# A transformer block on one core whose instruction order is chosen by another scheduler model

## The chip, the core and the metric

The kernel runs on one core of a Trainium2 chip. The metric is the device time of one execution in microseconds (us), from runs of the kernel alone. The engines of the core are TensorE (PE, matrix products; PEld is its weight load), VectorE (DVE), ScalarE (ACT), GpSimd (POOL) and SyncE (SP), which here issues nearly all DMA transfers. Each engine takes its instructions in the order of its own queue; an instruction that needs the result of another engine or of a transfer waits at the head of its queue.

## The reference

One layer of a hybrid encoder block, in float32, for one sequence of 2048 tokens with 1024 features:

```
xn = RMSNorm(h)
[mLSTM cols | MLA cols] = xn @ W_in
y_A = bidirectional chunkwise mLSTM   (4 heads x 128, chunks of 128)
y_B = multi-head latent attention     (4 heads, v dim 128)
h  += concat(y_A, y_B) @ W_out
h  += GatedMLP_with_centred_dwconv(RMSNorm(h))      (hidden size 2816)
h  += sigmoid(RMSNorm(h) @ W_g) * RMSNorm(p @ W_p)
out = RMSNorm(h)
```

The attention is a full softmax over 2048 keys for each of 4 heads and 16 tiles of 128 queries. The mLSTM runs over 16 chunks in both directions.

## The kernel before

Matrix products are done in several parts: a float32 operand is split into a rounded high part (a cast on ScalarE, L121) and the rest (a subtraction on VectorE, L124), and each product is a sum of products of such parts. So ScalarE and VectorE have two operations for each operand tile that PE uses.

The stages in the order of the program, with their place in the profiled execution:

- the input projection, 0 to 187 us (L134, L283); pairs of the convolution for the mLSTM's queries and keys, 187 to 425 (L544); the attention's queries, 425 to 480 (L860 on), whose order on PE is written by hand;
- the attention, 480 to 1180. For each head and tile of queries: four banks of scores on PE (L1162, tiles `bk`), their maxima on VectorE (L1195, `mx`), the negated maximum of the four (L1206, `nm`), the exponential of each bank on ScalarE with its row sums (L1212, `pe`, which frees the bank), transposes on PE (L1262, `tb`), the split of the transposed tile (L121 and L124, `pt`), and the product with the values (L1247, `ppv`). A bank is reused for the scores of a later tile once the exponential has read it. Between these steps the mLSTM's work is woven in by a generator: masks and states (L1017 to L1033, L1105 to L1154; `kk`, `cf`, `mk`, `mb`, `hy`, `qi`, `den`), and, at the end, the preparation of the output projection: its weights' splits (`op` from `opr`) and its first operands (`fw`, `fwd` from `yr`);
- the stream, 1180 to 2839: 84 pairs of 84 matmuls (L1740, results `fx`, `fy`, `fz`), 8 pairs for the output projection, 44 for the up projection, 24 for the down projection, 8 for the last gate. The last pair's order on PE, VectorE and ScalarE is written by hand (L1963).

The output of the attention is divided by the row sums only in `Out.scale` (L2007 to L2009): the reciprocals of the row sums (L1218, L1219, `gt`) are turned by PE (L1309, `tb`), copied by ScalarE (L1311, `ri`), stored (L1312, `ri_d`), loaded again for 128 partitions (L148, `rb`), and multiplied on VectorE onto the loaded attention output (L2003 loads `yr`, L2009 multiplies). L1695, L1696, L1713 and L1714 then form sums and differences of the `yr` tiles of a pair.

What sets the order: the code gives the instructions in program order, and a scheduler in the build re-orders them region by region before they are put into the engines' queues. It goes by its own model of how long an instruction takes. Left as written are the regions in `manual_schedule` (PE in the queries, L839; ScalarE in the last tile of the attention, L1340; PE, VectorE and ScalarE in the last pair of the stream, L1963) and single instructions pinned by `keep_in_program_order`. PE's instructions in the attention are tied together one by one:

```
def chained(self, ins):
    if self.link:
        self.tc.add_manual_dep(ins.ins, self.link.ins.name, mybir.DependencyInfo(
            mybir.DependencyClass.NoSync, mybir.DependencyReason.DATA), reason="chained")
    self.link = ins
```

so the scheduler may put other PE work (mLSTM, the stream's first products) between them, but not exchange them. The program order of an attention tile is a word list, "s" for a bank of scores, "X" for the negated maximum, "e" and "E" for an exponential, "t" for transposes and a split, "V" for the product with the values, and a dot for one step of the side work:

```
order = "s0 E1 . s1 E2 . . t0 t1 . . s2 . E3 . s3 . . X e0 t2 t3 . . V . .".split()
```

## Time and profile before

| | us |
|---|---|
| three runs, median (lowest to highest) | 2839.11 (2837.26 to 2842.2) |
| the profiled execution | 2840.89 |
| its span, first to last instruction | 2838.7 |
| PE busy, of the span | 2805.3 |
| VectorE busy | 2123.5 |
| ScalarE busy | 1574.3 |

The span is what the trace shows of the profiled execution; 2.2 us of that execution's time lie around it. The granted clock of PE was 0.998 of full speed on average. In the rows of a timeline the first number is the start in us from the beginning of the span, the second the duration; a bracket names the idle time ahead of the instruction and what ended it. In the table by windows, each engine's busy time is followed by its number of instructions, then come the granted clock of PE, the busy share of the DMA engines and GB/s.

### The profile page before, as it was taken

Reading aid. Unit: us, or ns where it says so; the run is one execution under the profiler, and the core shown is the slowest. Engines: PE = TensorE matmul, PEld = TensorE weight load, DVE = VectorE, ACT = ScalarE, POOL = GpSimd, SP = SyncE. Lnnn points to the kernel's source line nnn. Section 1 sums busy time; section 2 is a strip of 40 time slices with the busy share of each in tenths; the row PEclk is TensorE's granted clock in tenths of the full one; section 3 lists DMA queues with packets and bytes.
Section 4 is the critical chain, followed back from the end, with each engine's and each line's share of the span. In section 5 each row is a group of like instructions: output and inputs, shape, how many; then the busy total and the mean of one; then the engine's idle time right before and its main releaser. Section 6 shows DMA issues by size and latency. Waiting matters only on the chain.

```text
span 2838.7 us, 39453 instructions
## 1 busy us (share of the span) xinstructions
PE 2805.3 (99%) x13756; PEld 2349.9 (83%) x13756; DVE 2123.5 (75%) x3597; ACT 1574.3 (55%) x3068; POOL 209.3 (7%) x331
## 2 busy tenths in 40 slices
PE   9999999999999999999999999999999999999998
PEld 7888887888888888788888888888888788888787
DVE  4867866778777777877778778777778766676777
ACT  6346775566565556655655556655556332254665
POOL 2100000000000000044100000000000000011012
PEclk9999999999999999999999999999999999999999
DMA  8974756554433334588645445567776757575864
GB/s 299 289 236 120 216 183 216 190 175 140 136 129 106 99 99 128 160 255 288 224 154 195 163 163 187 184 208 237 227 239 215 223 195 234 170 267 200 294 199 163
DMA packets 444207, 553.73 MB, mean 195 GB/s; under 512 B 34500, under 2 KB 294632, under 8 KB 444008
## 3 DMA queue, kind: packets, MB, share of 16 engines
q1 hardware_dynamic: 444008, 551.21, 60.1%
q8 instruction: 108, 1.77, 0.3%
q14 instruction: 91, 0.75, 0.1%
HBM read 358.50 MB, written 192.61 MB: 194 GB/s over the span
## 4 chain that ended last, share of the span: by engine, by line
PE 90%; DVE 4%; DMA 3%; ACT 1%; issue 1%; SPq 0%; POOL 0%; POOLq 0%; ACTq 0%; DVEq 0%
PE fy L1740 22%; PE fz L1740 14%; PE fx L1740 14%; PE bk L1162 9%; PE bk L134 6%; PE ppv L1247 6%; PE tb L1262 4%; PE fy L544 3%; PE fx L544 2%; PE fz L544 2%; PE fs L134 1%; PE mb L1124 1%; PE mb L1029 1%; PE mb L1125 1%; DVE op L124 1%
## 5 line engine op out<-in xcount | busy, mean ns | idle before, releaser
L1740 PE MATMUL fz<-op,fw 128*128 128x512 f32 x1968 | 478.9, 392 | 2.0 <-DVE ug L1725 2.0
L1740 PE MATMUL fy<-op,fw 128*128 128x512 f32 x1968 | 475.3, 390 | 1.7 <-DVE xt L1725 1.4
L1740 PE MATMUL fx<-op,fw 128*128 128x512 f32 x1968 | 476.2, 390 | 0.0
L1740 PEld LDWEIGHTS fz<-op,fw 128*128 128x128 f32 x1968 | 368.6, 188 | 79.5 <-DVE ug L1725 2.4
L1740 PEld LDWEIGHTS fy<-op,fw 128*128 128x128 f32 x1968 | 368.6, 188 | 79.0 <-DVE xt L1725 1.8
L1740 PEld LDWEIGHTS fx<-op,fw 128*128 128x128 f32 x1968 | 368.2, 188 | 76.2
L1162 PE MATMUL bk<-kv,q_t 128*128 128x512 f32 x1280 | 334.8, 402 | 2.6 <-DVE q_t L1179 1.4
L1162 PEld LDWEIGHTS bk<-kv,q_t 128*128 128x128 f32 x1280 | 228.5, 188 | 45.5 <-ACT pe L1212 2.2
L121 ACT CAST pt<-tb 128x512 fp32r<-128x512 f32 x256 | 139.8, 588 | 183.5 <-PE tb L1262 183.2
L1740 PE MATMUL fy<-op,fwd 128*128 128x512 f32 (+1 forms) x984 | 237.9, 390 | 2.6 <-DVE fh L1725 1.5
L1195 DVE TENSOR_REDUCE mx<-bk 128x1 f32<-128x512 f32 x256 | 174.9, 686 | 58.2 <-PE bk L1162 55.3
L1740 PEld LDWEIGHTS fy<-op,fwd 128*128 128x128 f32 x984 | 182.6, 188 | 41.4 <-DVE fh L1725 1.9
L1247 PE MATMUL ppv<-pt,kv 128*128 128x512 f32 (+1 forms) x1024 | 198.7, 343 | 1.0 <-DVE pt L124 1.0
L1212 ACT ACTIVATE pe<-bk,nm 128x512 f32<-128x512 f32 x256 | 174.3, 697 | 34.5 <-DVE nm L1206 34.3
L124 DVE TENSOR_TENSOR pt<-tb,pt 128x512 fp32r<-128x512 f32 x256 | 167.8, 684 | 32.5 <-ACT pt L121 31.0
L124 DVE TENSOR_TENSOR fw<-fwr,fw 128x1024 fp32r<-128x1024 f32 x124 | 151.0, 1221 | 35.2 <-ACT fw L121 35.1
L1247 PEld LDWEIGHTS ppv<-pt,kv 128*128 128x128 f32 x1024 | 156.0, 188 | 20.3 <-DVE pt L124 1.2
L121 ACT CAST op<-opr 128x512 fp32r<-128x512 f32 x201 | 117.1, 619 | 75.2 <-PE fy L1740 12.7
L121 ACT CAST fw<-fwr 128x1024 fp32r<-128x1024 f32 x124 | 129.8, 1051 | 37.9 <-DVE fwr L1714 20.6
L124 DVE TENSOR_TENSOR op<-opr,op 128x512 fp32r<-128x512 f32 x201 | 131.5, 693 | 23.4 <-ACT op L121 23.3
L1262 PE MATMUL tb<-ident,pe 128*128 128x128 f32 x1024 | 135.5, 273 | 0.1
L121 ACT CAST fw<-hraw 128x1024 fp32r<-128x1024 f32 (+1 forms) x72 | 70.2, 980 | 114.8 <-PE fx L1740 58.9
(399 smaller groups left out, 4444.1 us busy)
## 6 DMA issues: line engine op xcount, KB each, us to landing
fwr<-in_w_up SPq DMA_DIRECT2D x66, 512.0 KB, 4.8
fh<-h_d SPq DMA_DIRECT2D x48, 512.0 KB, 4.2
h_d<-fh SPq DMA_DIRECT2D x48, 512.0 KB, 4.4
s_d<-fwr SPq DMA_DIRECT2D x44, 512.0 KB, 3.2
fws<-s_d SPq DMA_DIRECT2D x44, 512.0 KB, 3.5
rw<-row_d SPq DMA_DIRECT2D x32, 512.0 KB, 4.9
tw_d<-tsum SPq DMA_DIRECT2D x60, 256.0 KB, 5.1
opr<-tw_d SPq DMA_DIRECT2D x60, 256.0 KB, 4.6
```

Of the source, the lines that this page charges most:

```text
L121: nc.scalar.copy(hi, src)
L124: (sub or nc.vector).tensor_tensor(lo, src, _f(hi), op=ALU.subtract)
L134: mm = lambda *a, **k: self.nc.tensor.matmul(*a, **k, skip_group_check=more)
L544: nc.tensor.matmul(out, a[:, k * P:(k + 1) * P], parts[lo], start=first, stop=lo == 1 and k == 3, skip_group_check=more)
L1029: mm(ps[:, i, 0:129], kw[:, h, :], v1[:, h, :], start=True, stop=True)
L1124: mm(ps[:, i, 0:129], mk2[:, r, h, :], v1[:, h, :], start=True, stop=False)
L1162: mm = lambda *a, **k: self.chained(nc.tensor.matmul(*a, **k))
L1195: nc.vector.tensor_reduce(s.mx[:, kb:kb + 1], ps, axis=AX.X, op=ALU.max)
L1212: nc.scalar.activation(s.pe[:, kb % 2], s.banks[kb], AF.Exp, bias=s.nm, accum_out=s.rs[:, kb:kb + 1])
L1247: mm = lambda *a, **k: self.chained(nc.tensor.matmul(*a, **k))
L1262: self.chained(nc.tensor.transpose(t[:, j, :], s.p[kb][:, j * P:(j + 1) * P], self.ident))
L1740: nc.tensor.matmul(out, a[:, k * P:(k + 1) * P], parts[lo][:, cols], start=first, stop=lo == 1 and k == last, skip_group_check=more)
```

## The change

The tile framework's context is opened with another argument. It makes the scheduler go by the build's timeline simulation, another model of the machine, where it chooses which instruction comes next.

```diff
-    with _tile.TileContext(nc) as tc:
+    with _tile.TileContext(nc, schedule_with_timeline_sim=True) as tc:
         body(tc, d)
```

The instructions are the same, apart from one load of a table of ScalarE's functions that falls away (15 rather than 16). Regions ordered by hand keep their order. Everywhere else each engine's queue, SyncE's with the transfers included, is put in a new order, and with it the banks and buffers that rotate. Three places follow.

ScalarE near the end of the attention (`pe_11565` is the exponential of the first two banks of a tile, `ri_11606` the copy of the row sums' reciprocals, `mk_11664` masks of the mLSTM). Before:

```order
L1105 ACTIVATE mk_11664<-mk_11664,cols_2247 128x128 x4
L1145 ACTIVATE hy_11359,dsq_11553<-hy_11359 128x128 x4
L1105 ACTIVATE mk_11664<-mk_11664,cols_2247 128x128 x2
L121 CAST pt_11512<-tb_11513 128x4x128
L121 CAST pt_11520<-tb_11521 128x4x128
L1105 ACTIVATE mk_11664<-mk_11664,cols_2247 128x128 x2
L121 CAST op_12132<-opr_12009 128x512
L121 CAST pt_11567<-tb_11568 128x4x128
L121 CAST pt_11575<-tb_11576 128x4x128
L1212 ACTIVATE pe_11565,rs_11564<-bk_11495,nm_11562 128x512
```

Now:

```order
L121 CAST pt_11575<-tb_11576 128x4x128
L121 CAST q_t_11609<-q_t_11609 128x256
L1145 ACTIVATE hy_11359,dsq_11553<-hy_11359 128x128 x2
L1279 COPY ya_11601<-ppv_11473 128x256
L1311 COPY ri_11606<-tb_11604 32x128
L1105 ACTIVATE mk_11664<-mk_11664,cols_2247 128x128 x8
L121 CAST op_12132<-opr_12009 128x512
L1145 ACTIVATE hy_11359,dsq_11553<-hy_11359 128x128 x2
L1212 ACTIVATE pe_11565,rs_11564<-bk_11495,nm_11562 128x512
L1212 ACTIVATE pe_11565,rs_11564<-bk_11503,nm_11562 128x512
```

The mLSTM's masks and the copy of `ri` now stand ahead of the exponentials; before, the exponentials came directly behind the splits and the copy of `ri` behind them.

VectorE at the same place, from the split of `op_12132` on (`yr_11998` is the first attention output that is scaled, `rb_11994` its row sums' reciprocals; `mx_11611` the maxima of the next tile). Before, L2009 on `yr_11998` stood eight operations behind `nm_11704`, the negated maximum of that tile:

```order
L124 TENSOR_TENSOR op_12132<-opr_12009,op_12132 128x512
L1219 RECIPROCAL gt_82<-gt_82 128x1
L1148 TENSOR_TENSOR hy_11359<-hy_11359,rsr_11560 128x512
L124 TENSOR_TENSOR q_t_11609<-q_t_11609 128x256
L1195 TENSOR_REDUCE mx_11611<-bk_11612 128x1
L1284 TENSOR_TENSOR ya_11601<-ya_11601,ppv_11473 128x256
L1195 TENSOR_REDUCE mx_11611<-bk_11623 128x1
```

Now:

```order
L124 TENSOR_TENSOR op_12132<-opr_12009,op_12132 128x512
L2009 TENSOR_TENSOR yr_11998<-yr_11998,rb_11994 128x512
L1033 SCALAR_TENSOR_TENSOR cf_11490<-cf_11123,cols_2247,mb_11540 128x129 x2
L1148 TENSOR_TENSOR hy_11359<-hy_11359,rsr_11560 128x512
L1195 TENSOR_REDUCE mx_11611<-bk_11612 128x1
L1284 TENSOR_TENSOR ya_11601<-ya_11601,ppv_11473 128x256
L124 TENSOR_TENSOR op_12043<-opr_12001,op_12043 128x512
L1195 TENSOR_REDUCE mx_11611<-bk_11623 128x1
```

L2009 has moved ahead of all four maxima of the tile. Some 60 rows further on, `nm_11945` (the negated maximum of a later tile) likewise has operations of the output projection ahead of it that stood behind it: `fw1_12161`, `fwd_12195`, L1695, L1696 and L1713 on the `yr` tiles, `fw1_12248`, `op_12132`, `op_12171` and `pt_11848`.

VectorE at the end of the attention (`pt_12301` is the last split that the attention's last product needs, `yr_12594` an attention output of a later pair). Before:

```order
L124 TENSOR_TENSOR pt_12293<-tb_12361,pt_12293 128x4x128
L124 TENSOR_TENSOR op_12368<-opr_12219,op_12368 128x512
L2009 TENSOR_TENSOR yr_12508<-yr_12508,rb_12510 128x512
L124 TENSOR_TENSOR pt_12301<-tb_12379,pt_12301 128x4x128
L1218 TENSOR_REDUCE gt_82<-rs_12290 128x1
```

Now:

```order
L2009 TENSOR_TENSOR yr_12508<-yr_12508,rb_12510 128x512
L124 TENSOR_TENSOR pt_12293<-tb_12361,pt_12293 128x4x128
L124 TENSOR_TENSOR op_12368<-opr_12219,op_12368 128x512
L124 TENSOR_TENSOR fwd_12561<-yr_12508,fwd_12561 128x512
L2009 TENSOR_TENSOR yr_12594<-yr_12594,rb_12596 128x512
L1695 TENSOR_TENSOR yr_12508<-yr_12508 128x512
L124 TENSOR_TENSOR pt_12301<-tb_12379,pt_12301 128x4x128
```

L2009 on `yr_12594`, which before stood 37 rows further on, is now ahead of `pt_12301`. On SyncE the load of its `rb_12596` and that of `rb_12724` have moved ahead of the operand loads `opr_12415` and `opr_12419`.

## The prediction

> **What bounds the kernel now.** The page comes first: the span, the busy shares of the engines, and the chain that ended last.

> ```profile
> span 2838.7 us, 39453 instructions
> ...
> PE 2805.3 (99%) x13756; PEld 2349.9 (83%) x13756; DVE 2123.5 (75%) x3597; ACT 1574.3 (55%) x3068; POOL 209.3 (7%) x331
> ...
> PE 90%; DVE 4%; DMA 3%; ACT 1%; issue 1%; SPq 0%; POOL 0%; POOLq 0%; ACTq 0%; DVEq 0%
> ```

> TensorE (PE) is busy 99% of the span, and 90% of the chain is its own work. No matmul is added or removed, so the time can only change through PE's idle time (and its clock). VectorE (DVE) at 75% is next. Then the table by stage, PE's busy time first in each row, and the sum.

> ```profile
> 1100.00:1110.00 10.00, 10.00 (x62) 8.80 (x61) 7.75 (x21) 8.32 (x29) 1.20 (x2) 1.00 0.40 122
> 1110.00:1120.00 10.00, 10.00 (x66) 8.87 (x65) 8.66 (x18) 6.14 (x16) 0.00 (x0) 1.00 0.64 224
> 1140.00:1150.00 10.00, 10.00 (x57) 8.29 (x56) 9.68 (x19) 6.16 (x15) 0.00 (x0) 1.00 0.53 158
> ```
> ```profile
> 1400.00:2200.00 800.00, 799.82 (x3529) 662.14 (x3528) 618.14 (x751) 445.57 (x633) 0.00 (x0) 1.00 0.60 196
> 2800.00:2838.70 38.70, 29.45 (x142) 24.68 (x140) 28.43 (x44) 17.81 (x39) 7.86 (x17) 0.92 0.43 144
> sum 2838.70, PE 2805.32 PEld 2349.92 DVE 2123.46 ACT 1574.26 POOL 209.25; mean PE 187.02 PEld 156.66 DVE 141.56 ACT 104.95 POOL 13.95
> ```

> PE is idle 2838.70 - 2805.32 = 33.4 us in all, 38.70 - 29.45 = 9.25 of them in the last stretch, which is ordered by hand. So an order can win at most about 24 us. It can lose far more: at the end of attention PE has no idle time only because VectorE, busy 7.75 to 9.68 of each 10 us, hands over in time. Last, the view of PE's waits, the total per line and the longest one:

> ```profile
> PE mb L1029 <- DVE kk L1022: 2.5, 1, 2.5
> PE fz L1740 <- DVE ug L1725: 2.0, 1, 2.0
> PE fy L1740 <- DVE xt L1725: 1.9, 2, 1.4
> PE mb L1153 <- DVE hy L1148: 1.8, 4, 0.9
> PE fy L1740 <- DVE fh L1725: 1.5, 1, 1.5
> ```

> No single wait is large; the kernel loses little anywhere.

> **The change part by part.** The instructions stay (one table load of ScalarE fewer); only their places in the queues move. I went along the queues and compared how much work now stands ahead of each hand-over to PE. In the steady part of the stream (1400 to 2200) products and conversions move together, and I cost them at nothing: VectorE idles 800 - 618 = 182 us there, and that cover would have to vanish first. In most of the attention VectorE's work between two hand-overs shifts by several us, but earlier banks cover it; nothing again. Two places are left where the new order looks worse, and two where it looks better.

> *Term A, 1108 to 1130.* The rows of ScalarE, PE, VectorE and SyncE there:

> ```profile
> 1101.30 1.28 ACT L1105 ACTIVATE mk<-mk,cols 128x128 f32<-128x128 f32 x4
> ...
> 1109.04 0.70 ACT L1212 ACTIVATE pe<-bk,nm 128x512 f32<-128x512 f32 x1
> ...
> 1111.96 0.25 ACT L1311 COPY ri<-tb 32x128 f32<-32x128 f32 x1
> ```
> ```profile
> 1111.09 0.27 PE L1309 MATMUL tb<-ident,gt 128*32 128x128 f32 x1
> 1111.12 2.56 PE L1162 MATMUL bk<-kv,q_t 128*128 128x512 f32 x10
> ...
> 1122.58 2.47 PE L1162 MATMUL bk<-kv,q_t 128*128 128x512 f32 x10
> ```
> ```profile
> 1119.47 0.15 DVE L1206 TENSOR_REDUCE nm<-mx 128x1 f32<-128x4 f32 x1
> ...
> 1121.66 0.68 DVE L2009 TENSOR_TENSOR yr<-yr,rb 128x512 f32<-128x512 f32 x1
> ```
> ```profile
> 1112.23 0.34 SPq L1312 DMA_DIRECT2D ri_d<-ri  x1
> ...
> 1114.83 0.38 SPq L148 DMA_DIRECT2D rb<-ri_d  x1
> ```
> ```profile
> DMA to landing us min/median/max: 3.3/4.7/6.2
> ```

> First ScalarE. Before, the exponential (1109.04) ran as soon as its maximum was there; now the copy of `ri` (needs PE's L1309), eight L1105 (2 x 1.28 = 2.6 us), one split and two square sums (about 1 us) stand ahead of it. With L1309 ending at 1111.4 and four matmuls of L1125/L1124 moved ahead of it (0.9), the copy ends at about 1112.5, the exponential starts at about 1116. PE's scores at 1111.12 need the bank that it frees, so PE stands for about 3 us. Then VectorE. Its L2009 on `yr_11998`, at 1121.66 before, is now ahead of four maxima and of `nm` (1119.47). It waits for two loads of `rb`, which follow the store of `ri` at 1112.23. In the old order the first was issued at 1114.83; in the new one no store stands between, so about 1114.2, and with the median landing of 4.7 it arrives at 1118.9. VectorE stands from about 1112 to then, with some 8.7 us of work (nine operations of 0.68, two of 1.29 or less) left before `nm`: 1128 rather than 1119.5. PE's scores at 1122.58 wait for the exponential behind it, now at about 1128.5 to 1129: 6 us late, the 3 us above within them. **A = +6**; bounds 0 (the stall is only a shift of idle time) and +9 (all of `nm`'s delay).

> [...]

> *Term B, 1131 to 1160.*

> ```profile
> 1143.19 0.15 DVE L1206 TENSOR_REDUCE nm<-mx 128x1 f32<-128x4 f32 x1
> ...
> 1144.58 1.21 DVE L124 TENSOR_TENSOR fw<-yr,fw 128x1024 fp32r<-128x1024 f32 x1
> ```
> ```profile
> 1143.43 0.69 ACT L1212 ACTIVATE pe<-bk,nm 128x512 f32<-128x512 f32 x1 [0.48 <-DVE nm L1206]
> ```
> ```profile
> 1144.26 2.58 PE L1162 MATMUL bk<-kv,q_t 128*128 128x512 f32 x10
> ```

> `nm` at 1143.19 feeds the exponential at 1143.43, whose end (1144.12) frees the bank for PE's scores at 1144.26: a slack of 0.14 us. Nine operations of the out projection's preparation, behind this `nm` before, stand ahead of it now: seven of about 0.68 and two of 1.21, 7.2 us by their rows, while one of 0.68 goes behind it. Since neighbouring rows overlap a little I take 5.5 of the 6.5, less about half a us that earlier hand-overs give. **B = +5**; bounds 0 (VectorE makes up for it in PE's new idle time from A) and +8.

> *Term C, 1175 to 1210, attention's last product and the first out-projection pairs.*

> ```profile
> 1177.81 0.69 DVE L2009 TENSOR_TENSOR yr<-yr,rb 128x512 f32<-128x512 f32 x1
> 1178.42 0.68 DVE L124 TENSOR_TENSOR pt<-tb,pt 128x512 fp32r<-128x512 f32 x1
> ...
> 1204.83 0.69 DVE L2009 TENSOR_TENSOR yr<-yr,rb 128x512 f32<-128x512 f32 x1
> ```
> ```profile
> 1179.20 1.63 PE L1247 MATMUL ppv<-pt,kv 128*128 128x512 f32 x8
> ```

> The L2009 of `yr_12594`, at 1204.83 before, now stands ahead of the split `pt` at 1178.42. Its load waits for the L2009 that ends at 1178.5, and needs 4.7 (up to 6.2): the split moves to 1183.8 at least, and PE's product at 1179.20 with it, +5. About 12 matmuls pulled ahead on PE cover 2.9. On SyncE a second `rb` load that waits for this L2009 stands ahead of the operand loads of the next pairs; they come some 3 us later. **C = +4**; bounds 0 (more matmuls pulled ahead) and +10 (no cover, operands late as well).

> *Term D, better places.* The wait of 2.0 on `ug` goes: the product that it needs is 11 us earlier. It costs more than itself:

> ```profile
> 2205.00:2210.00 5.00, 3.86 (x18) 2.85 (x16) 5.00 (x8) 2.49 (x5) 0.00 (x0) 1.00 0.83 256
> 2210.00:2215.00 5.00, 4.17 (x11) 3.30 (x12) 3.71 (x6) 3.14 (x5) 0.00 (x0) 0.66 0.82 268
> ```
> ```profile
> 2204.62 2.88 PE L1740 MATMUL fx<-op,fw 128*128 128x512 f32 x12
> ...
> 2210.84 4.60 PE L1740 MATMUL fz<-op,fw 128*128 128x512 f32 x12 [1.98 <-DVE ug L1725]
> ```

> After that wait the granted clock was 0.66, and twelve matmuls took 4.60 instead of 2.88: 1.7 more. So 3.7 are to be had, and 1.5 from the wait on `fh` (2660 to 2668). Against that stand about 2 us at 495 to 510, where the mLSTM chain of products and copies is now packed closer on PE than its copies allow. **D = -3**; bounds -8 (half of the other waits go as well) and +2.

> *Term E, the clock.* The same rows give the price of a stall's aftermath, 1.7 us. Other waits as long (2.5 on `kk`) left the clock alone, so of the three or four stalls of A to C I count one and a half: **E = +2.5**; bounds 0 and +7.

> [...]

> Sum against the profiled execution (2840.89, span 2838.7): 2840.9 + 6 + 5 + 4 - 3 + 2.5 = 2855.4. It was 1.8 above the median of the three runs, 2839.11, so I predict **2854**.

> **The rivals.**
> - *No change.* VectorE idles a quarter of the span, and what is pulled ahead is done and need not be done later; A to C shrink to the loss of one bank, 1 to 2 each, and D pays for them: 2840.9 + 4 - 3 - 1.8 = 2840. For it: most of the attention shows that slack. Against: the slack of 0.14 at 1144. That the change did nothing is excluded: the listings of VectorE's queue, some 3,100 rows each, differ in 4,793 lines.
> - *Faster.* The mechanism is at PE's own waits, not at VectorE: the new order spaces producer and consumer wider. It decides if half of the 24 us of idle time that isn't hand-ordered is closed, while the `rb` loads land before VectorE gets to L2009, that is if some 7 us of its other work runs in front of it by then. A and B are then under 1: 2839.1 - 12 + 3 = 2830. Against: in the new queue that work stands behind L2009, not ahead.
> - *Far slower.* The head-of-line waits seen in A recur all over the attention: 64 softmax steps (256 maxima in fours), and if one in four loses 1.4 us, as the longest wait on `xt` does, 22 more: 2876. For it: the conversions of the queries now stand closer behind their loads. Against: those have several us of slack in the middle of the attention.

> **How the numbers follow.** Forecast 0.52, with its own range 2844 to 2866; no change 0.18; faster 0.13; far slower 0.17. The range leaves out the lower half of the faster case and the upper part of the far slower one, about 2 in 10: 2833 to 2880. A measurement of this kernel tells about 0.2% (5.7 us) from no change; the forecast's case gives a little to "same": faster 0.13, same 0.19, slower 0.68.

> **What would show it.** Right: PE idle in the windows 1110 to 1130 and 1140 to 1165 rises from nothing to some 5 us each, with L2009 shown as waiting for a DMA of `rb` and PE's L1162 for the exponential of L1212; 1170 to 1210 loses 4 more than before; the wait on `ug` is gone; 1400 to 2200 stays full. Wrong: those windows stay full (A and B are hidden), or idle time turns up in windows of the attention from 500 to 1080 that I cost at nothing, or VectorE waits in the stream.

## The result and the profile after

| | before | after |
|---|---|---|
| median (lowest to highest), us | 2839.99 (2837.26 to 2842.2) | 3006.72 (3002.34 to 3010.41) |
| ratio to before, 95% interval | | 1.0593 [1.058, 1.0605] |
| span of the profiled execution | 2838.7 | 3008.5 |
| PE busy / idle in the span | 2805.3 / 33.4 | 2864.6 / 143.9 |

The change makes the kernel 167 us slower, far outside the range that was given (2833 to 2880). The page of the kernel after: span, busy shares, and the chain by engine.

```profile
span 3008.5 us, 39537 instructions
...
PE 2864.6 (95%) x13756; PEld 2388.5 (79%) x13756; DVE 2122.4 (71%) x3597; ACT 1572.8 (52%) x3067; POOL 218.2 (7%) x331
...
PE 74%; DMA 9%; DVE 7%; ACT 3%; issue 2%; SPq 0%; POOL 0%; ACTq 0%; POOLq 0%; DVEq 0%
```

VectorE and ScalarE do the same work in the same time as before; PE has 110.5 us more of idle time, and the same 13756 matmuls are busy for 59.3 us more. Together that is the 169.8 us between the spans. Next the table by windows, of the kernel after: each engine's busy time, then (behind POOL's) PE's granted clock.

```profile
600.00:800.00 200.00, 165.42 (x934) 140.52 (x933) 122.43 (x290) 87.21 (x243) 9.41 (x14) 0.88 0.38 119
800.00:1000.00 200.00, 180.57 (x1043) 155.42 (x1042) 132.95 (x317) 101.75 (x295) 14.97 (x21) 0.93 0.33 103
1000.00:1180.00 180.00, 155.72 (x873) 133.93 (x873) 112.83 (x276) 87.92 (x257) 14.11 (x20) 0.91 0.29 90
...
1600.00:1800.00 200.00, 200.00 (x884) 165.62 (x883) 155.31 (x196) 105.41 (x148) 0.00 (x0) 1.00 0.51 172
```

and the first of these windows before:

```profile
600.00:800.00 200.00, 199.73 (x1250) 175.98 (x1249) 158.32 (x386) 120.47 (x348) 15.89 (x24) 1.00 0.42 135
```

From 600 to 800, where PE was full, it now does 934 instead of 1250 matmuls, and up to 1180 its granted clock is 0.88 to 0.93. The stream (1600 to 1800) is as full as before. So the loss is in the middle of the attention, the place that the prediction had costed at nothing; idle time there is the sign that it had named for being wrong. The view of PE's waits names it:

```profile
PE mb L1029 <- DVE hy L1136: 34.2, 15, 3.3
PE mb L1029 <- DVE cf L1033: 10.5, 15, 0.7
PE ppv L1247 <- DVE ya L1284: 9.3, 3, 5.4
PE mb L1029 <- DVE kk L1022: 8.2, 5, 2.6
...
PE mb L1029 <- DVE cb L1033: 7.1, 6, 4.0
```

Fifteen waits on `hy` and fifteen on `cf`: one of each in every chunk of the mLSTM's forward loop that updates a state. One such place on PE after (start, duration; in brackets the idle time before and what ended it):

```profile
883.31 0.39 PE L1125 MATMUL mb<-cb,qi 128*128 128x129 f32 x2
883.45 1.30 PE L1247 MATMUL ppv<-pt,kv 128*128 128x512 f32 x6
887.83 1.20 PE L1029 MATMUL mb<-v,kk 128*128 128x129 f32 x4 [3.08 <-DVE hy L1136]
889.73 1.23 PE L1029 MATMUL mb<-v,kk 128*128 128x129 f32 x4 [0.70 <-DVE cf L1033]
890.61 3.93 PE L1162 MATMUL bk<-kv,q_t 128*128 128x512 f32 x10
```

and the state products of a chunk before:

```profile
638.95 0.61 PE L1029 MATMUL mb<-v,kk 128*128 128x129 f32 x4
639.32 1.40 PE L1162 MATMUL bk<-kv,q_t 128*128 128x512 f32 x5
640.56 0.49 PE L1262 MATMUL tb<-ident,pe 128*128 128x128 f32 x3
640.88 0.61 PE L1029 MATMUL mb<-v,kk 128*128 128x129 f32 x4
```

L1029 doesn't use `hy` or `cf`; neither is an operand of it. But every product of the mLSTM (L1017, L1029, L1110, L1124, L1125, L1153) writes a tile `mb` from a pool of PSUM with a single buffer, `("ml", 1)` in `run`. So the next product waits until the last one's result has been read out of that bank, here by VectorE: in L1136 for `hy`, in L1033 for `cf`. At the place above the read by L1136 ends at 887.69 and L1029 starts at 887.83; that by L1033 ends at 889.68, and the second pair starts at 889.73. Before, five matmuls of the attention or more stood between the two pairs of L1029 of a state, and the bank was read while they ran (by L1033 from 640.09 to 640.69, between the pairs at 638.95 and 640.88). After, the two pairs are next to each other on PE. The listings of PE's order, counted over the forward and the backward loop (matmuls of other kinds between the two pairs of L1029 of one state):

```
            states   fewest between   none between   median
before        30           5                0            9
after         30           0               20            0
```

This table is about the wait on `cf`. The larger one, on `hy`, is of the first pair, which follows the last L1125 on the bank. In the traces 18 other matmuls or more stand between these two before (23 in the median), and after it depends on the chunk: in ten of the 15 chunks there are 0 to 6, and the wait is 2.6 to 3.3 us; in the other five there are 15 to 25, and it is 0.4 to 0.8.

What a stall costs behind itself is to be seen in the rows too: ten matmuls of L1162 take 3.93 us at 890.61, where the granted clock is 0.50 up to 893.59, and 2.49 to 2.56 at 903.86 to 918.05, where it is 1.00. The backward loop is hit in another way. After, its last chunks were left over, and stand in a row with no work of the attention between them:

```profile
620.46 0.66 PE L1017 MATMUL mb<-ident,kTb 128*128 128x128 f32 x4 [0.70 <-DVE cb L1033]
622.52 0.71 PE L1029 MATMUL mb<-v,kk 128*128 128x129 f32 x4 [1.40 <-DVE kk L1022]
623.93 1.23 PE L1029 MATMUL mb<-v,kk 128*128 128x129 f32 x4 [0.70 <-DVE cb L1033]
625.86 1.12 PE L1017 MATMUL mb<-ident,kTb 128*128 128x128 f32 x4 [0.70 <-DVE cb L1033]
```

Where the time went in the span: the starts of PE's matmuls of L134, L544, L1162, L1247 and L1740, the k-th of them in the trace after less the k-th before. The differences of that delay, from stretch to stretch (times are those of before; the delay jumps at some of the boundaries, so a row is good to some 1.5 us):

```
 before, us      delay added, us    what runs there
   0 -  480          +6.9           input projection, pairs, queries
 480 -  606         -12.8           backward loop (part of it deferred)
 606 -  666         +47.8           its rest, in a row on PE
 666 - 1043         +74.3           forward loop
1043 - 1162         +38.9           forward loop's last chunks, end of the attention
1162 - 1263          +6.2           last product, first pairs of the stream
1263 - 2823          +8.1           stream
```

### The profile page after: what moved, and what is told of

The parts are those of the page before. It is cut to its first block, busy times and chain, and to the rows that moved or that the text cites. A ratio compares the mean times of both kernels' runs of the same rounds, so it can differ in the third digit from the quotient of the medians.

```text
span 3008.5 us, 39537 instructions
## 1 busy us (share of the span) xinstructions
PE 2864.6 (95%) x13756; PEld 2388.5 (79%) x13756; DVE 2122.4 (71%) x3597; ACT 1572.8 (52%) x3067; POOL 218.2 (7%) x331
## 4 chain that ended last, share of the span: by engine, by line
PE 74%; DMA 9%; DVE 7%; ACT 3%; issue 2%; SPq 0%; POOL 0%; ACTq 0%; POOLq 0%; DVEq 0%
PE fy L1740 20%; PE fz L1740 13%; PE fx L1740 13%; PE bk L1162 10%; PE ppv L1247 5%; PE tb L1262 3%; PE fy L544 2%; PE fs L134 1%; PE mb L1029 1%; PE fx L544 1%; PE fz L544 1%; DMA q_t<-q_d 1%; DMA opr<-tw_d 1%; PE mb L1124 1%; DVE op L124 1%
## 5 line engine op out<-in xcount | busy, mean ns | idle before, releaser
L1740 PE MATMUL fx<-op,fw 128*128 128x512 f32 x1968 | 491.9, 391 | 5.2 <-ACT fw L121 3.1
L1740 PE MATMUL fy<-op,fw 128*128 128x512 f32 x1968 | 485.3, 390 | 5.8 <-ACT fy L1856 2.4
L1740 PE MATMUL fz<-op,fw 128*128 128x512 f32 x1968 | 484.6, 391 | 0.9 <-ACT op L129 0.4
L1740 PEld LDWEIGHTS fy<-op,fw 128*128 128x128 f32 x1968 | 368.8, 188 | 84.5 <-ACT fy L1856 3.5
L1740 PEld LDWEIGHTS fx<-op,fw 128*128 128x128 f32 x1968 | 368.2, 188 | 82.3 <-ACT fw L121 3.9
L1740 PEld LDWEIGHTS fz<-op,fw 128*128 128x128 f32 x1968 | 368.3, 188 | 79.3 <-ACT op L129 1.5
L1162 PE MATMUL bk<-kv,q_t 128*128 128x512 f32 x1280 | 345.6, 414 | 5.6 <-ACT pe L1212 4.7
L1162 PEld LDWEIGHTS bk<-kv,q_t 128*128 128x128 f32 x1280 | 240.5, 198 | 53.8 <-ACT pe L1212 6.1
L1740 PE MATMUL fy<-op,fwd 128*128 128x512 f32 (+1 forms) x984 | 238.7, 390 | 2.1 <-DVE fh L1725 1.9
L124 DVE TENSOR_TENSOR pt<-tb,pt 128x512 fp32r<-128x512 f32 x256 | 168.3, 685 | 86.1 <-ACT pt L121 83.9
L1247 PE MATMUL ppv<-pt,kv 128*128 128x512 f32 (+1 forms) x1024 | 210.4, 356 | 11.6 <-DVE ya L1284 9.3
L1740 PEld LDWEIGHTS fy<-op,fwd 128*128 128x128 f32 x984 | 183.7, 188 | 40.9 <-DVE fh L1725 2.1
L1212 ACT ACTIVATE pe<-bk,nm 128x512 f32<-128x512 f32 x256 | 173.2, 692 | 73.4 <-DVE nm L1206 73.4
L1247 PEld LDWEIGHTS ppv<-pt,kv 128*128 128x128 f32 x1024 | 163.9, 197 | 33.5 <-ACT op L121 5.6
L124 DVE TENSOR_TENSOR fw<-fwr,fw 128x1024 fp32r<-128x1024 f32 x124 | 151.0, 1222 | 12.0 <-ACT fw L121 11.9
L124 DVE TENSOR_TENSOR fwd<-fwr,fwd 128x512 fp32r<-128x512 f32 x56 | 38.8, 693 | 156.1 <-ACT fwd L121 156.1
L124 DVE TENSOR_TENSOR op<-opr,op 128x512 fp32r<-128x512 f32 x201 | 131.5, 686 | 24.1 <-ACT op L121 23.5
L1262 PE MATMUL tb<-ident,pe 128*128 128x128 f32 x1024 | 136.9, 273 | 2.0 <-DVE pt L124 2.0
```

Source lines behind the costliest of these rows:

```text
L124: (sub or nc.vector).tensor_tensor(lo, src, _f(hi), op=ALU.subtract)
L1162: mm = lambda *a, **k: self.chained(nc.tensor.matmul(*a, **k))
L1212: nc.scalar.activation(s.pe[:, kb % 2], s.banks[kb], AF.Exp, bias=s.nm, accum_out=s.rs[:, kb:kb + 1])
L1247: mm = lambda *a, **k: self.chained(nc.tensor.matmul(*a, **k))
L1262: self.chained(nc.tensor.transpose(t[:, j, :], s.p[kb][:, j * P:(j + 1) * P], self.ident))
L1740: nc.tensor.matmul(out, a[:, k * P:(k + 1) * P], parts[lo][:, cols], start=first, stop=lo == 1 and k == last, skip_group_check=more)
```

## The experiments

Two theories stood against each other. P: the loss is PE's order, mLSTM products put next to each other on one bank. V: it is VectorE's and ScalarE's order, which make `hy` and `cf` late. Times below are medians, and the kernel before ran beside them at 2835.6 to 2838.4.

**PE's order undone.** The mLSTM's products are tied into the attention's chain, so that PE keeps the program order there; once under the new model, once under the old.

```diff
-        mm = nc.tensor.matmul
+        mm = lambda *a, **k: self.chained(nc.tensor.matmul(*a, **k))
...
-                nc.tensor.transpose(pk[:, h, :], kT[:, h, :], self.ident)
+                self.chained(nc.tensor.transpose(pk[:, h, :], kT[:, h, :], self.ident))
...
-                nc.tensor.transpose(pt[:, h, :], hh[:, h, :], self.ident)
+                self.chained(nc.tensor.transpose(pt[:, h, :], hh[:, h, :], self.ident))
```

> The new scheduler model, but on PE the mLSTM's products are tied into the attention's chain and so keep their program order; every other engine and stage stays with the new order's rules. Theory P (the loss is PE's order: mLSTM products that share the one bank ml are put next to each other on PE and each waits for VectorE to read the bank): the 46 us lost between 600 and 665 and some 95 of the 110 lost after it come back, 2850 to 2880 us, and PE's waits on hy, cf, cb and kk (64 us together after the change) fall under 15. Theory V (VectorE's and ScalarE's own order makes hy and cf late): it stays above 2960, and the waits on hy and cf remain.

> The same tie under the old scheduler model, as a control for the tie itself. Theory P: 2840 us within 8, since the old order spreads these products anyway. Theory V says the same; if it is slower by over 10, the program order is not a neutral stand-in and the run before has to be read against this one.

New model with the tie: 2896.07 us, ratio 1.0206 [1.0191, 1.0221]; 111 of the 167 us are back, and the granted clock is 0.997. Old model with the tie: 2858.01, 1.0071 [1.0054, 1.0088]. What is left of the waits on `hy` in the first of them (L1002 is the tied product's line):

```profile
PE mb L1153 <- DVE hy L1148: 8.3, 8, 2.3
PE mb L1002 <- ACT hy L1134: 5.2, 8, 1.6
PE mb L1002 <- DVE hy L1136: 4.9, 5, 1.6
PE mb L1002 <- DVE cb L1033: 4.6, 3, 2.6
```

So PE's order in the attention is two thirds of the loss. Both expectations were missed in part: the time is above theory P's 2880, and these four rows alone hold 23 us of waits, where it asked for under 15; the program order isn't neutral (20 us slower than the old model's own order), and with the same order on PE the new model is still 38 us slower than the old.

**Parts of it undone.** Only the backward loop's products tied, and only the forward states' L1029.

```diff
-                    mm(ps[:, i, 0:129], kw[:, h, :], v1[:, h, :], start=True, stop=True)
+                    ins = mm(ps[:, i, 0:129], kw[:, h, :], v1[:, h, :], start=True, stop=True)
+                    if r:
+                        self.chained(ins)
```

(the first also ties the transposes of L1017; the second has `if not r`)

> The new model, only the backward pass's products (L1017 and L1029 of the backward states) tied into the attention's chain. Theory P: the 46 us at 600 to 665 come back and nothing else, 2950 to 2970 us. Theory V: within 10 of 3007.

> The new model, only the forward states' products (L1029 in the forward loop, 15 times two pairs) tied into the attention's chain. Theory P: the wait on hy (34 us in 15 waits) and most of the wait on cf (10.5 in 15) go, with the clock that they cost, 70 to 95 us in all: 2912 to 2937. Theory V: within 15 of 3007, the wait on hy only moves to another product.

The backward tie gave 2975.24 us (a single run, as the next), 31.5 less and 5 above the expected range: about the net of its two stretches in the table (47.8 - 12.8 = 35). The expectation had the 46 alone, without the 13 that deferring had won. How much of it is the bank's and how much the chain's own (`kk` is an operand of L1029) wasn't taken apart. The forward tie was a miss with the wrong sign: 3035.19. L1029 no longer sits next to its twin, but the products that were still free now crowd in front of it. L1126 and L1138 are here what L1124 and L1136 are elsewhere:

```profile
PE mb L1029 <- DVE hy L1138: 45.8, 15, 3.2
PE mb L1126 <- DVE hy L1138: 23.1, 15, 1.9
PE mb L1126 <- ACT hy L1136: 18.4, 9, 3.5
```

Fixing one of the products moves the pile to the next: this model's order doesn't keep them apart, wherever they stand.

**The price, made in the old order.** From the old model with the tie (2858 us), the forward states' products are put behind the last L1125 and next to each other; the steps of side work between them go behind. Then the same order on PE, with those products' results in the transposes' pool of two banks.

```diff
-            yield from pause(9 if (r, j) == (1, 0) else 3)
+            yield from pause(9 if (r, j) == (1, 0) else 3 if r else 0)
...
-                yield from pause(2)
+                yield from pause(2 if r else 0)
...
-                    yield from pause(3)
+                    yield from pause(0 if r and hp and c < NT - 1 else 3)
...
                 yield from state(0, c, kk, v1, cf, cn)
+                yield from pause(10)
```

The second kernel adds:

```diff
-                ps = mbank([P, 2, 256])
+                ps = mbank([P, 2, 256]) if r else self.ptr.tile([P, 2, 256], F32, name="mb", tag="tr")
```

> The old model with the tie (2858 us), and in the forward loop the two pairs of state products L1029 put directly behind the last L1125 and next to each other, as the new order has them; the steps of side work that stood between come behind. Theory P1 (the price is the turnaround of the one bank ml: L1029 waits until VectorE's hy has read the bank, the second pair until cf has): 15 times 3.1 + 0.7 us of waits and about 2.5 for slow products and the clock, 2858 + 95 = 2953 us, between 2920 and 2970, with waits of L1029's line on hy near 3 us, 15 times. Theory V (only together with the new order of VectorE and ScalarE is the bank read so late): under 2885.

> As the run before (the same order on PE), but the forward state products write to the pool of the transposes (two banks) instead of ml. Theory P1: the wait on hy goes, since the bank of hy is no longer needed; what is left is the transposes' banks, 2858 to 2890 us. Rival (the state products wait for their operand kk or for something else that comes late, the bank is only what the trace names): within 15 of the run before.

Packed: 2947.66 us, 90 more than the 2858 that it was made from. Packed with the other banks: 2860.44. The first row is of the packed kernel, the second of the one with other banks, where no row of L1002 on `hy` L1136 is left among the first seven:

```profile
PE mb L1002 <- DVE hy L1136: 46.0, 17, 3.2
```
```profile
PE tb L1263 <- DVE cf L1033: 4.5, 9, 0.8
```

(L1263 is L1262, one line down through the edit.) And the place itself, of the packed kernel and then of the one with other banks:

```profile
882.21 1.20 PE L1002 MATMUL mb<-v,kk 128*128 128x129 f32 x4 [2.93 <-DVE hy L1136]
884.11 1.23 PE L1002 MATMUL mb<-v,kk 128*128 128x129 f32 x4 [0.70 <-DVE cf L1033]
```
```profile
882.63 1.06 PE L1002 MATMUL mb<-v,kk 128*128 128x129 f32 x8
884.53 0.66 PE L1263 MATMUL tb<-ident,pe 128*128 128x128 f32 x4 [0.84 <-DVE cf L1033]
```

That settles the mechanism for the forward loop's state products: 2.93 + 0.70 us of waiting in the packed kernel, as after the change (3.08 + 0.70), come with the order on PE, under the old model's rules for all other engines; and nearly all of the 90 us goes when the same products, in the same order on PE, have another bank. 90 us in 15 chunks are 6.0 each. By the traces of the packed kernel and of the one that it was made from, PE's idle time rises by 47.9 us and the busy time of the same matmuls by 40.1: 3.2 and 2.7 in a chunk.

**Other banks under the new model.** The same pool for all state products, without a tie:

> The new model without a tie, all state products (backward and forward) in the transposes' pool. Theory P1: the waits of L1029 on hy (34 us) and on cf and cb go, and at least 60 of the 167 us come back, under 2945; products that are still next to each other on the bank ml (L1017, L1110, L1124) keep theirs. Rival: as in e3, where tying one kind of product moved the pile to the next, the new order piles up others, above 2985.

2950.07 us in a single run: 57 come back, 5 us short of the expectation. The waits of L1029 on `hy` have left the head of the list, and another stands there, on the scores' banks:

```profile
PE bk L1162 <- ACT pe L1212: 20.4, 15, 3.9
```

The transposes' banks are shared now, and the model's order may be another one too; which of them makes the exponentials late isn't shown.

**The places that the prediction named.** L2009 tied behind the negated maximum and behind the split, where it had stood before. The lines that aren't shown only keep these two instructions, `nms[-4]` and `lastpt`.

```diff
...
-        if i == -8:
-            self.b.tc.keep_in_program_order(a)
+        if i in (-8, -6):
+            to = self.b.nms[-4] if i == -8 else self.b.lastpt
+            self.b.tc.add_manual_dep(a.ins, to.ins.name, mybir.DependencyInfo(
+                mybir.DependencyClass.NoSync, mybir.DependencyReason.DATA), reason="scale")
```

> The new model; only the L2009 of yr_11998 and yr_11995 tied behind the negated maximum nm_11704, and that of yr_12594 behind the split pt_12301: terms A and C of the prediction undone. If these terms were right in size: 3007 - 6 - 4 - 1.7 for a stall's clock = 2995 us, and VectorE's wait of 5.7 on the load of rb before L2009 is gone. If they are hidden behind the mLSTM's waits: within 4 of 3007.

3000.3 us (2996.07 to 3004.24), against 3006.72: some 6 less, half of what was expected, with ranges that overlap. The kernel before ran 4.4 us faster beside this run than beside the change (2835.58 against 2839.99), so the 6 us aren't clear of noise. VectorE's wait is there after the change, and gone here (L2010 is L2009, one line further down through the edit):

```profile
1255.22 0.69 DVE L2009 TENSOR_TENSOR yr<-yr,rb 128x512 f32<-128x512 f32 x1 [5.73 <-DMA rb<-ri_d]
```
```profile
1264.13 1.28 DVE L2010 TENSOR_TENSOR yr<-yr,rb 128x512 f32<-128x512 f32 x2
```

The two profiled executions are 8.6 us apart. By the delay of PE's matmuls between them some 2 us are won around L2009 on `yr_11998`, where one is lost again some 20 us on, and 3.4 around L2009 on `yr_12594`, whose wait of 2.42 us for `rb` is gone too. About 4 of the 8.6 turn up near the end of the stream, and are not explained by this edit.

**What is left with the same order on PE.** Tied on PE, and VectorE in program order in the attention as well, under both models:

```diff
-        self.attend(self.mlstm())
+        with self.tc.manual_schedule(engines={mybir.EngineType.DVE}):
+            self.attend(self.mlstm())
```

> The new model with PE's tie (2896 us) and, in the attention's region, VectorE kept in program order too. Theory V2 (the 38 us that are left between the two tied runs are VectorE's order in the attention, 13 in the forward loop and 12 at its end): within 15 of the control with the old model. Rival (ScalarE's order, the transfers' order, or the stages outside): it stays 25 or more above the control.

> The control: the old model with PE's tie and VectorE in program order in the attention. No theory says how good that order is; 2850 to 2900 us.

2891.07 and 2866.81 us: the gap falls from 38 to 24, where the theory asked for 15 at most and the rival for 25 at least: neither holds. Of these 14 us only 5 are a gain of the new model's kernel (2896.07 to 2891.07); the other 9 are a loss of the old one (2858.01 to 2866.81), whose own order of VectorE was better than the program order. By the delays, holding VectorE narrows the gap in the forward loop between 666 and 1043 (from 9 to some 6) and most at the end of the attention and the stream's start, 1043 to 1263 (from some 13 to 2). What stays is 2 or 3 by 544 us, 12 in the two loops up to 1043, 2 at the end of the attention and 7 in the stream. So over a third of the gap between the models is VectorE's order in the attention; the rest belongs to other engines' queues and other stages, and wasn't taken apart further.

**Does the old order pay for its one bank?** The kernel before with all state products in the transposes' pool:

```diff
-                ps = mbank([P, 2, 256])
+                ps = self.ptr.tile([P, 2, 256], F32, name="mb", tag="tr")
```

> The kernel before, with the state products in the transposes' pool. If the one bank ml costs the old order anything, its waits of L1029 on hy (0.4 us) and most of the one on kk (2.5 us) go: 0 to 3 us faster. If the transposes' banks are tighter than ml, up to 10 us slower. Theory P1 says only that the old order pays little for the bank.

2852.47 us, ratio 1.005 [1.0036, 1.0064]: 14 slower, more than either branch of the expectation. With the products spread as the old order has them, the one bank was the better place for them, as far as the model didn't change its order with the pool. No kernel here beat the one before, and none of the runs points to one that would.

## Why the prediction was wrong

**The bound** was read rightly: PE's own work, little to win (33.4 us of idle time), much to lose. The direction, slower, held; its size was a tenth of the real one (+14 against +167).

**The step that failed** is the sentence ahead of the terms: "In most of the attention VectorE's work between two hand-overs shifts by several us, but earlier banks cover it; nothing again." It held, in the main, for the scores, which have four banks (their waits on the exponential are 4.7 us in all after the change). The mLSTM's products have one bank. I compared how much work stood ahead of each hand-over on VectorE and ScalarE, but not how far apart two products on the same bank stood on PE. The order listings hold that answer: 20 of 30 pairs with nothing between. The price was readable too, if roughly, from VectorE's rows before: for the wait on `cf` one reading (L1033, 0.60) and the hand-over, and for that on `hy` the 3.3 us from the start of L1128 at 633.20 to the end of L1136 at 636.46, where the operations on the bank take 1.0 and others stand between them.

**Term D** had the mechanism in it, at the wrong place and size: "about 2 us at 495 to 510, where the mLSTM chain of products and copies is now packed closer on PE than its copies allow". It is 35 net in the backward loop and most of 74 + 39 in the forward loop. I looked at the chain where the old trace showed a wait (2.5 on `kk`), and took the other 14 chunks of each loop for covered. The gain in D came in part: no wait on `ug` is left in PE's list, but one of 2.1 (`fx` on `fy`) stands in nearly the same place, so that the delay falls by 2 there, against the 3.7 that I took. The wait on `fh` is still there (1.9, before 1.5), and others (`fx` on `fw`, 3.1 in two) more than give back the rest.

**Term A** (+6): VectorE's wait was right, its way to PE was not. L2009 waits 5.73 us for `rb`, where I had nearly 7. On PE the windows around it, and the two waits there that are not the last chunk's L1029:

```profile
1240.00:1255.00 15.00, 11.28 (x62) 9.41 (x60) 6.73 (x20) 9.03 (x30) 3.18 (x4) 0.89 0.55 164
1255.00:1270.00 15.00, 11.11 (x56) 9.07 (x56) 11.18 (x22) 6.58 (x15) 0.00 (x0) 0.89 0.39 127
```
```profile
1257.09 0.66 PE L1153 MATMUL mb<-ident,hy 128*128 128x128 f32 x4 [1.91 <-DVE hy L1148]
1261.11 1.26 PE L1262 MATMUL tb<-ident,pe 128*128 128x128 f32 x8 [1.99 <-DVE pt L124]
```

7.6 us of idle time from 1240 to 1270, of which 3.7 are the last chunk's waits on `hy` and `cf` (3.0 + 0.7): 3.9 for the rest. No product of scores waits for the exponential there, as I had it; PE waits for `hy` and for `pt`. And the 3.9 are not all L2009's: with L2009 put back, the wait on `hy` is gone, but that on `pt` is 3.3, and some 2 us are won. That A comes near its size is in good part luck.

**Term B** (+5): 7.6 us of idle time from 1285 to 1300 (15.00 - 7.40):

```profile
1285.00:1300.00 15.00, 7.40 (x38) 6.10 (x37) 13.85 (x32) 7.07 (x20) 1.70 (x2) 0.77 0.47 147
```

0.9 of it is before a product of the mLSTM (L1124 on `hy`), 5.4 before L1247, and 1.3 before scores that wait for the exponential. It isn't `nm` that is late first, as I had it, but the sum L1284, which stands behind the same operations of the output projection and frees the bank of the next product with the values:

```profile
1291.48 0.68 DVE L1696 TENSOR_TENSOR yr<-yr 128x512 f32<-128x512 f32 x1
...
1292.68 0.41 DVE L1284 TENSOR_TENSOR ya<-ya,ppv 128x256 f32<-128x256 f32 x1
```
```profile
1293.24 4.47 PE L1247 MATMUL ppv<-pt,kv 128*128 128x512 f32 x16 [5.42 <-DVE ya L1284]
```

**Term C** (+4): PE is idle for 40 - 33.86 = 6.1 us from 1330 to 1370, and was for 3.2 in 1170 to 1210 before: about +3. The mechanism was there: L2009 on `yr_12594` waits 2.42 us for `rb` ahead of the split, PE's product waits 1.3 for the split and the first pairs 1.8 for `op`, and both waits are gone where this L2009 is put back.

```profile
1330.00:1370.00 40.00, 33.86 (x157) 27.10 (x156) 28.89 (x46) 18.50 (x31) 0.00 (x0) 1.00 0.65 211
```

**Term E** (+2.5): the aftermath of a stall was a matter of one and a half stalls in my sum. With over 30 waits PE's busy time rises by 59.3 us, a third of the loss. The trace records the granted clock. Between 670 and 1300 it is at 0.5 behind these stalls for 3.41 or 6.83 us, and from 623.94 to 668.31, where the backward loop's products stand in a row, it is at 0.5 all the time. The slow stretches from 804.84, 845.80, 886.76 and 927.72 start 40.96 us apart, twelve times 3.41. Windows of 3.41 us around the stall at 887.83:

```profile
883.35:886.76 3.41, 1.41 (x10) 0.99 (x8) 3.10 (x7) 2.81 (x10) 1.40 (x2) 1.00 0.42 122
886.76:890.17 3.41, 1.64 (x6) 1.37 (x7) 1.46 (x7) 2.88 (x12) 1.20 (x2) 0.50 0.57 202
890.17:893.59 3.42, 3.42 (x11) 2.86 (x11) 1.66 (x4) 0.65 (x2) 0.00 (x0) 0.50 0.64 230
```

In the first of them PE is idle for 2.0 us, and in the second, which has the wait of 0.70, for 1.8. Between 670 and 1300 of this trace each of the 15 slow stretches follows such a window with 1.8 to 3.3 us of idle time (two windows with 1.9 have none behind them). Nine of them last for two windows, and there the first has 0.7 us of idle time or more; six last for one, with 0.5 or less in it. Of the stretches at 1084.7 and 1207.6, both two windows long, the small wait on `cf` is nearly all the idle time that the first window has (0.8 and 0.7), so my estimate is that it doubled the slow time there. In the kernel before, the 1.98 on `ug` lay in one window, and the clock fell; the 2.5 on `kk` lay across a window's end, 1.7 and 0.9, and it did not; but it did behind the window from 449.87 to 453.28, with 1.6. So no run here shows one idle time from which on the clock falls. In all PE is busy for 106.1 us at the half clock after the change, and for 6.8 before. Before, twelve matmuls lost 1.7 us around the slow stretch from 2211.15 to 2214.57 (4.60 instead of 2.88), half of its length; so half of the difference of 99.3, 50 us, is an estimate of what the clock cost of the 59.3.

**The rival "far slower"** (0.17) had the right sign and stage and another cause, waits on the queries' conversions, and at 2876 it was far too small as well. The range failed with it: its upper end came from the terms that I had found and from this rival, not from what the places that I had taken as covered could cost at most.

## What to carry to other kernels

When only an order changes, list for each buffer with one copy its users in the new order, and ask what stands between two of them on the engine that fills it; distance on the producer's queue is what hid the reader's latency here, and busy shares didn't show it. Where the trace ascribes a wait to an instruction whose result isn't an operand, look for a buffer that both use. Where a loop repeats a small wait, price it with its number of rounds and with the slow clock behind it before calling it covered.
